# Up's first six blocks interleaved with the row factors, four blocks' weight sums formed in DRAM, and the key scaling moved later

## The chip, the cores and the metric

The kernel runs on one core of one Trainium2 chip. TensorE (PE, with PEld for its weight loads), VectorE (DVE), ScalarE (ACT), GpSimd (POOL) and SyncE (SP) each work through a queue of their own, in order; sixteen DMA engines move data between DRAM and SBUF and within DRAM. SP and POOL here mostly issue transfers. The metric is the device time of one execution, in microseconds (us): 2825.24 us as the median of three runs before the change (2822.13 to 2829.9).

## The reference

One residual block of a decoder, sequence 512, width 2048, everything in float32:

```python
h = rms_norm(x, norm1_g);  z = h @ w_in                    # 2048 -> 9152 columns
o_rw  = rwkv7_mix(token_shift(z[..., :shift]), ...)        # 16 heads of 64, a recurrence over the tokens
o_att = swa_attention(q, k, v, ...)                        # 16 heads, window 128, sinks
x = x + (sigmoid(zg_rw) * (o_rw @ w_branch[:1024]) + sigmoid(zg_att) * (o_att @ w_branch[1024:])) @ w_out
x = x + conv_ffn(rms_norm(x, norm2_g), w_up, conv_w, conv_b, w_down)

def conv_ffn(h, w_up, conv_w, conv_b, w_down):
    u = h @ w_up                                           # 2048 -> 11264
    c = causal 3-tap convolution of u along the tokens, + conv_b
    val, gate = split(c);  return (silu(gate) * val) @ w_down
```

In the RWKV part the keys are scaled to unit length per head: `kk = (k * k_k) / max(sqrt(sum(kk^2)), 1e-12)`, and `kk` and `kk * a` enter the recurrence; the output takes a bonus from `sum(r * k * r_k)`, which does not use `kk`.

## The kernel before

**Precision.** Each float32 product is made of three matmuls. A weight tile `raw` is split into `whi` (an ACT copy, rounded) and `wlo` (a DVE subtraction), the other factor likewise, and PE forms hi·hi, hi·lo and lo·hi. So each 128x1024 weight tile costs one ACT and one DVE instruction besides its load, and PE has 24 matmuls for it in Up.

**Stages in order.** (1) `x` is normalised and transposed. (2) The input projection runs through column tiles (`ztile`, `project`, lines 255 to 257), with attention work first and then eight RWKV pairs (of two heads each). For each pair `early` projects k, r and v and prepares the factors, `late` runs the recurrence (`psG`, `psU`, `psS`), `final` makes the output; gate tiles fill PE in between. (3) The branch projection ends with `factors` and `store_factors`, which write the row factors of the next stage to DRAM. (4) The output projection "o", (5) Up with the convolution, and (6) Down "dn".

**Seven products instead of eight.** Stages 4 to 6 use a Strassen-Winograd scheme: the rows' side and the weights' side are cut in halves, and seven products of sums replace eight. On the weights' side of "o" and "dn" the sums are made in DRAM during earlier stages: `sums_along` takes a job, lets SP copy one quarter to a scratch tensor (SP, pinned in order), and POOL then adds the other by an accumulating transfer. For Up, block f (0 to 43, 256 output columns as two 128-column tiles) needs the products P1, P2, P7, P6, P5, Q4, P3. Their weights are a quarter (P1, P2, Q4) or a sum: s3 for P7 and s1 for P5 are made in SBUF by an SP load and an accumulating POOL transfer, while P6 = a11 + s1 and P3 = P6 + a12 are made by DVE additions in the tile `a` (`sums`, line 1069).

**Rows' side of Up.** After "o" the four quarters q11, q12, q21, q22 of the new x are normalised and transposed. The first two (from the upper rows) become the factors b11 and b21 while "o" still runs. The lower rows come only with the last product of "o": `taken_out` (line 974), squares and sums on ACT, `diagonals` (a 128x128 diagonal of row scales), then `transposed` (line 1024) for q12 and q22. From them come t3 = q22 - q12, t1 = q11 - q12, t2 = -t1 - q22, t4 = -t2 - q21 and b22 = q22, each a 128x2048 DVE operation, and each then split into hi (ACT, line 1040) and lo (DVE, line 1041).

**What sets the order in Up.** The list `steps` gives PE's products. `run(i)` issues the split of the weights of step i+2 (`prep`, lines 1075 and 1076), then the 24 matmuls of step i, then the output instructions (`out`, lines 1109 to 1113). `pin` keeps these in the order of the program; the split of row factors was not pinned, so the scheduler placed it. `whi` and `wlo` have rings of three tiles, so a split can start only when PE has left the product three steps back. Weight tiles have a ring of six (`raw`) and one of two (`a`); a load goes out when the tile's last reader has been prepared. SP's loads and POOL's accumulating transfers each stand in one queue, together with the copies and sums for "dn" that `sums_along` still spreads over Up. Before, the list was: P1, P2, P7 of blocks 0 to 3; then blocks 0 and 1 with P6, P5, P3, Q4 interleaved; the same for 2 and 3; then block by block. P1 and P2 of blocks 0 to 3 are kept in `t1` and in the upper half `Z` of the PSUM tile until the upper rows' output can be placed.

Of the kernel before, what the change touches and what calls it, by code (L numbers as in the profile page):

```python
# [134 lines left out]
def block_kernel(ctx: ExitStack, tc: tile.TileContext, d: Dims, a: dict, out: bass.AP):  # L135
# [18 lines left out]

    ident = const.tile([P, P], F32, name="ident")
# [60 lines left out]
    jobs = []  # L216
    for w in ("o", "dn"):
        for kinds in (
            (("s1", (1, 0), (1, 1)), ("s3", (0, 0), (1, 0))),
            (("s2", "s1", (0, 0)),),  # L220
            (("s4", "s2", (0, 1)),),
        ):
            jobs += [(w, k, c, q) for c in range(NB[w]) for q in range(2) for k in kinds]
    def sums_along():

        if not jobs:
            return lambda: None
        w, (n, first, second), c, q = jobs.pop(0)
        dst = sum_d[w][n][c][q]
        pin(sync.dma_start(dst, quarter(w, first, c)[q], max_dma_last_dim=4096))  # L230
        return lambda: pool.dma_start(dst, quarter(w, second, c)[q], accum_op=ALU.add, max_dma_last_dim=4096)
# [46 lines left out]
    if True:  # L278
# [188 lines left out]
        with ExitStack() as pr:  # L467
# [67 lines left out]
            def early(p):  # L535
# [5 lines left out]

                acc = ztile(d.c_k + p * P)
# [10 lines left out]
                dve.tensor_tensor(kk, kk, rb, op=ALU.mult)  # L553


# [17 lines left out]
                ta = wtile("lw")  # L573
# [219 lines left out]
            for p in range(NP):  # L793
# [3 lines left out]
                final(p, lt)  # L797
                for _ in range(GATES_PER_PAIR * NK // 16):
                    emit_gate()
# [70 lines left out]
    hp = hps.enter_context(tc.tile_pool(name="hhlC", bufs=3, side="right", reuse_waits="tile"))  # L870
# [92 lines left out]
    def taken_out(i, acc, xr, scale, done):  # L963
        ci, tj, sign = PRODUCTS[i][4]
        last = i in (3, 4, 5, 6)
        for t in range(NT // 2):
            for e in range(NQW):
# [5 lines left out]
                else:  # L973
                    dve.scalar_tensor_tensor(x, acc[t][e], sign * scale, x, op0=ALU.mult, op1=ALU.add)
# [6 lines left out]
    bq = {n: [bqp.tile([P, KH, TH], F32R, name=f"{n}{i}") for i in range(2)] for n in ("b11", "b21")}  # L981
    NCC = d.D // S
# [32 lines left out]
    def transposed(tps, i, q, dg=None):  # L1015
# [11 lines left out]
        for k in range(KH):  # L1027
            src, g = pss[k // 2][:, k % 2], col("n2g", i * KH + k)
            dst = q[:, 2 * k // KH, k % (KH // 2) * TH : (k % (KH // 2) + 1) * TH]
            if k % 2:  # L1030
                dve.tensor_scalar(dst, src, g, None, op0=ALU.mult)
            else:
                act.activation(dst, src, AF.Copy, scale=g)
# [4 lines left out]
    def split_q(n, q):  # L1038
        hi, lo = (halves(x) for x in bq[n])
        act.activation(hi, q, AF.Copy)  # L1040
        dve.tensor_tensor(lo, q, hi.bitcast(F32), op=ALU.subtract)
# [3 lines left out]


    NPRE = 4

    class Block:
# [3 lines left out]
        def __init__(self, f):  # L1053
            self.f, self.w, self.hl = f, {}, {}

        def load(self, n):
            f, w = self.f, self.w
            at = {"p11": (0, 0), "p12": (0, 1), "a11": (0, 0), "a12": (0, 1), "s3": (0, 0), "s1": (1, 0), "a22": (1, 1)}
            w[n] = raw_tile("a11", 2) if n in ("a11", "p11") else raw_tile()
            sync.dma_start(w[n], a["w_up"][(f, *at[n])])  # L1060
            if n in ("s3", "s1"):
                pool.dma_start(w[n], a["w_up"][f, 1, int(n == "s1")], accum_op=ALU.add)

        def sums(self, n):

            w = self.w
            if n in ("P6", "P3"):
# [3 lines left out]
        def parts(self, n):  # L1071
            one = "ap"[self.f < NPRE]
            t = self.w[{"P1": one + "11", "P2": one + "12", "P7": "s3", "P6": "a11", "P5": "s1", "Q4": "a22", "P3": "a11"}[n]]
            hi, lo = (hlp.tile([P, WC], F32R, name=f"w{e}", tag=f"w{e}") for e in ("hi", "lo"))
            pin(act.activation(hi, t, AF.Copy))  # L1075
            pin(dve.tensor_tensor(lo, t, hi.bitcast(F32), op=ALU.subtract))  # L1076
            self.hl[n] = hi, lo

        def mm(self, n):
# [6 lines left out]
            ps = getattr(self, {"P2": "Z", "P7": "Y", "Q4": "Y"}.get(n, "X"))  # L1086
            start = n in ("P1", "P7") or n == "P2" and self.f >= NPRE
# [8 lines left out]
        def out(self, n):  # L1096
            X, Y, Z = self.X, getattr(self, "Y", None), self.Z
            if n == "P7":
                return
# [292 lines left out]
```

## Time and profile before

| what | value |
|---|---|
| median of the runs | 2825.24 us (2822.13 to 2829.9) |
| the profiled execution's own time | 2823.84 us |
| its span, first to last instruction | 2822.0 us |
| PE busy | 2768.1 us, 98% of the span |
| DVE busy | 1994.0 us, 71% |
| ACT busy | 1350.7 us, 48% |
| POOL busy | 225.3 us, 8% |
| moved by DMA | 607.04 MB, 215 GB/s over the span |

PE is busy nearly always, so time can come only from the places where it is not, or from making it do less. A row of a window view gives, for a stretch of time, each engine's busy time in it, the granted TensorE clock (1.00 is full speed) and the share of the DMA engines' time in use; what is missing from PE's busy time there is a gap. "[0.88 <-DVE x L974]" after an instruction says how long its engine stood idle before it and what ended the wait. The chain is the path of work that ended last, one piece after the other.

### The profile page before, as it was taken

What the parts mean: (1) busy time and instruction counts of PE and PEld (TensorE: products, weight loads), DVE (VectorE), ACT (ScalarE), POOL (GpSimd) and SP (SyncE); (2) the same over time, 40 slices, a digit from 0 to 9 for tenths busy, and PEclk for the clock granted to TensorE, in tenths of its full rate; (3) what the DMA queues carried; (4) which work ended last, traced back from release to release, by engine and by line L of the source; (5) the groups of instructions that cost most, each with busy time, mean ns of one, the idle gap of its engine ahead of it and who ended that gap; (6) DMA issues with size and microseconds to landing.
All of it is one profiled execution on the core that took longest, in us unless ns stands there. A gap on an engine that the chain in (4) does not pass through costs nothing.

```text
span 2822.0 us, 45987 instructions
## 1 busy us (share of the span) xinstructions
PE 2768.1 (98%) x17466; PEld 2401.8 (85%) x17466; DVE 1994.0 (71%) x3456; ACT 1350.7 (48%) x2274; POOL 225.3 (8%) x299
## 2 busy tenths in 40 slices
PE   7999999999999999999999899999999999999999
PEld 5777787787778778888888899999999999888887
DVE  4588677777777774545678777777777778655555
ACT  4255445544544553322465545554545455444444
POOL 0001000000000001011010010111010101000000
PEclk9999999999999999999999999999999999999999
DMA  7855676666666667888777888888888888877875
GB/s 219 224 158 163 176 183 163 173 170 162 172 165 178 154 168 220 237 258 286 234 251 220 223 224 238 243 228 219 239 237 229 221 241 231 312 243 241 257 256 188
DMA packets 223726, 607.04 MB, mean 215 GB/s; under 512 B 24448, under 2 KB 44560, under 8 KB 222480
## 3 DMA queue, kind: packets, MB, share of 16 engines
q1 hardware_dynamic: 156096, 432.64, 47.5%
q0 software_dynamic: 36064, 132.14, 24.6%
q10 hardware_dynamic: 31344, 39.31, 4.1%
q8 instruction: 137, 2.24, 0.3%
q14 instruction: 85, 0.70, 0.1%
HBM read 554.38 MB, written 174.40 MB: 258 GB/s over the span
## 4 chain that ended last, share of the span: by engine, by line
PE 88%; DVE 5%; ACT 2%; DMA 2%; issue 1%; ACTq 0%; SPq 0%; DVEq 0%; POOLq 0%
PE X L1093 17%; PE X L960 11%; PE acc L256 10%; PE acc L255 10%; PE acc L257 10%; PE Y L960 9%; PE Y L1093 8%; PE Z L1093 4%; PE psS L744 1%; PE psG L735 1%; PE bulk L627 1%; DVE wlo L241 1%; PE bulk L677 1%; DMA raw<-in_w_dn_dram 1%; ACT whi L240 1%
## 5 line engine op out<-in xcount | busy, mean ns | idle before, releaser
L256 PE MATMUL acc<-xlo,whi 128*128 128x512 f32 x1152 | 462.9, 402 | 0.0
L255 PE MATMUL acc<-xhi,whi 128*128 128x512 f32 x1152 | 460.1, 399 | 1.9 <-DVE xlo L301 1.9
L257 PE MATMUL acc<-xhi,wlo 128*128 128x512 f32 x1152 | 461.7, 401 | 0.0
L953 DVE TENSOR_TENSOR wlo<-raw,whi 128x1024 fp32r<-128x1024 f32 x210 | 256.9, 1224 | 207.1 <-ACT whi L952 204.1
L240 ACT ACTIVATE whi<-raw 128x512 fp32r<-128x512 f32 x352 | 220.1, 630 | 364.1 <-PE acc L256 287.9
L952 ACT ACTIVATE whi<-raw 128x1024 fp32r<-128x1024 f32 x210 | 222.8, 1061 | 289.7 <-PE X L960 146.4
L241 DVE TENSOR_TENSOR wlo<-raw,whi 128x512 fp32r<-128x512 f32 x352 | 241.4, 689 | 158.5 <-ACT whi L240 145.2
L1093 PE MATMUL X<-b,whi 128*128 128x256 f32 x1472 | 269.1, 283 | 2.3 <-DVE u L1113 0.9
L1076 DVE TENSOR_TENSOR wlo<-raw,whi 128x1024 fp32r<-128x1024 f32 x176 | 214.9, 1222 | 76.6 <-ACT whi L1075 76.1
L1093 PE MATMUL X<-t,whi 128*128 128x256 f32 x1408 | 258.7, 284 | 9.6 <-DVE u L1113 9.1
L1093 PE MATMUL Y<-t,whi 128*128 128x256 f32 x1408 | 257.1, 283 | 0.0
L255 PEld LDWEIGHTS acc<-xhi,whi 128*128 128x128 f32 x1152 | 217.3, 189 | 42.2 <-DVE xlo L301 2.2
L256 PEld LDWEIGHTS acc<-xlo,whi 128*128 128x128 f32 x1152 | 217.4, 189 | 40.2 <-issue 1.7
L257 PEld LDWEIGHTS acc<-xhi,wlo 128*128 128x128 f32 x1152 | 217.3, 189 | 38.3 <-issue 0.9
L1075 ACT ACTIVATE whi<-a 128x1024 fp32r<-128x1024 f32 x132 | 139.4, 1056 | 215.9 <-DVE a L1069 214.2
L1093 PEld LDWEIGHTS X<-b,whi 128*128 128x128 f32 x1472 | 229.5, 192 | 3.1 <-issue 2.4
L1093 PEld LDWEIGHTS X<-t,whi 128*128 128x128 f32 x1408 | 220.7, 193 | 10.2 <-DVE u L1113 6.6
L1093 PEld LDWEIGHTS Y<-t,whi 128*128 128x128 f32 x1408 | 219.6, 192 | 0.0
L1093 PE MATMUL X<-b,wlo 128*128 128x256 f32 x736 | 208.4, 283 | 2.1 <-DVE wlo L1076 2.1
L1076 DVE TENSOR_TENSOR wlo<-a,whi 128x1024 fp32r<-128x1024 f32 x132 | 161.7, 1225 | 67.6 <-ACT whi L1075 66.9
L1093 PE MATMUL X<-t,wlo 128*128 128x256 f32 x704 | 199.8, 284 | 0.3 <-DVE wlo L1076 0.3
L1093 PE MATMUL Y<-t,wlo 128*128 128x256 f32 x704 | 199.2, 283 | 0.0
(352 smaller groups left out, 5786.1 us busy)
## 6 DMA issues: line engine op xcount, KB each, us to landing
raw<-in_w_up_dram SPq DMA_DIRECT2D x180, 512.0 KB, 5.3
raw<-in_w_z_dram SPq DMA_DIRECT2D x288, 256.0 KB, 4.2
s_dn<-in_w_dn_dram POOLq DMA_DIRECT2D x88, 512.0 KB, 6.6
raw<-in_w_up_dram POOLq DMA_DIRECT2D x88, 512.0 KB, 8.4
raw<-s_dn SPq DMA_DIRECT2D x88, 512.0 KB, 3.9
raw<-in_w_dn_dram SPq DMA_DIRECT2D x66, 512.0 KB, 3.9
a<-in_w_up_dram SPq DMA_DIRECT2D x48, 512.0 KB, 5.3
s_dn<-in_w_dn_dram SPq DMA_DIRECT2D x44, 512.0 KB, 5.3
```

The costliest lines, as they stand in the source:

```text
L240: act.activation(hi, raw, AF.Copy)
L241: dve.tensor_tensor(lo, raw, hi.bitcast(F32), op=ALU.subtract)
L255: pe.matmul(acc, whi[:, j], xhi[:, k], start=first, stop=False)
L256: pe.matmul(acc, whi[:, j], xlo[:, k], start=False, stop=False)
L257: pe.matmul(acc, wlo[:, j], xhi[:, k], start=False, stop=last)
L627: pe.matmul(ps[:, j * 2 * P : (j + 1) * 2 * P], BKK[:, n0 + j], BAR[:, n0 + j].rearrange("p h a c -> p (h a c)"), start=True, stop=True)
L952: act.activation(whi, wr, AF.Copy)
L953: dve.tensor_tensor(wlo, wr, whi.bitcast(F32), op=ALU.subtract)
L960: pe.matmul(dst, l[:, q, ts], r[:, es], start=fst and j == 0, stop=lst and j == 2, skip_group_check=True)
L1075: pin(act.activation(hi, t, AF.Copy))
L1076: pin(dve.tensor_tensor(lo, t, hi.bitcast(F32), op=ALU.subtract))
L1093: pin(pe.matmul(ps, l[:, k], r[:, k], start=start and k + i == 0, stop=last and i == 2, skip_group_check=True))
```

## The change

1. **Sums in DRAM for blocks 0 to 3.** Sixteen new jobs (`up_jobs`: s3, s1, P6, P3 for each block) use the same `sums_along`: one at the beginning of each `early`, one after each `final`. Each is an SP copy of 512 KB in DRAM and an accumulating POOL transfer of 512 KB. P3's copy reads the finished P6, and P6's addition reads s1. Up then loads the finished sums, and the accumulating transfers of s3 and s1 and the DVE additions for P6 and P3 fall away for these four blocks.
2. **Another order of Up's steps**, with P6 of blocks 0 to 3 right after P7, and blocks 4 and 5 interleaved with each other and with the end of blocks 2 and 3. Blocks 2 and 3 take P5 and P3 into `Z` (`apart`).
3. **The row factors written out in that order**, pinned: `high` and `low` replace `split_q` and stand between the steps; t1 comes after t3 and t2. The split of b21 is moved from the end of "o" into Up, and the last weight split before Up is divided (`lo1` after `taken_out`).
4. **Another place for the factor tiles of "o"**: the pool `hhlC` has two tiles, used for the first two; the others (`hhlO`, three tiles) lie on the left side of SBUF, in memory that the branch stage used.
5. **RWKV pairs:** the multiplication of `kk` by its scales `rb` comes after the split of `rk` instead of right after the scales are asked for, so what does not use `kk` stands ahead of it; `ta` and `rk` live in other tiles.

```diff
+    NPRE = 4
+    up_d = {(f, n): dram.tile([P, DH], F32, name=f"{n}_u{f}") for f in range(NPRE) for n in ("s3", "s1", "P6", "P3")}
...
+    jobs, up_jobs = [], []
+    for f in range(NPRE):
+        w, t = a["w_up"][f], {n: up_d[f, n] for n in ("s3", "s1", "P6", "P3")}
+        up_jobs += [(t["s3"], w[0, 0], w[1, 0]), (t["s1"], w[1, 0], w[1, 1]), (t["P6"], w[0, 0], t["s1"]),
+                    (t["P3"], t["P6"], w[0, 1])]
...
+    def sums_along(jobs=jobs):
         if not jobs:
             return lambda: None
+        dst, first, second = jobs.pop(0)
+        pin(sync.dma_start(dst, first, max_dma_last_dim=4096))
+        return lambda: pool.dma_start(dst, second, accum_op=ALU.add, max_dma_last_dim=4096)
...
+                sums_along(up_jobs)()
                 acc = ztile(d.c_k + p * P)
...
                 rb = head_rows(wk, bulk(), rs, "lg")
-                dve.tensor_tensor(kk, kk, rb, op=ALU.mult)
...
-                dve.tensor_tensor(kb, kk, ta, op=ALU.mult)
                 rk = wtile("lw")
                 dve.scalar_tensor_tensor(rk, rz, col("r_k", p), k2, op0=ALU.mult, op1=ALU.mult)
-                rkl = [wk.tile([P, S], F32R, name=f"rk{e}", tag="gn" if e else "lg") for e in range(2)]
+                rkl = [wk.tile([P, S], F32R, name=f"rk{e}", tag="rhl" if e else "dd") for e in range(2)]
                 split(*rkl, rk)
+                pin(dve.tensor_tensor(kk, kk, rb, op=ALU.mult))
+                dve.tensor_tensor(kb, kk, ta, op=ALU.mult)
...
-    hp = hps.enter_context(tc.tile_pool(name="hhlC", bufs=3, side="right", reuse_waits="tile"))
+    hp0 = hps.enter_context(tc.tile_pool(name="hhlC", bufs=2, side="right", reuse_waits="tile"))
...
+    hp = hps.enter_context(tc.tile_pool(name="hhlO", bufs=3, reuse_waits="tile"))
...
+    def high(n, q, pin=pin):
+        pin(act.activation(halves(bq[n][0]), q, AF.Copy))
+
+    def low(n, q, pin=pin):
         hi, lo = (halves(x) for x in bq[n])
-        act.activation(hi, q, AF.Copy)
-        dve.tensor_tensor(lo, q, hi.bitcast(F32), op=ALU.subtract)
+        pin(dve.tensor_tensor(lo, q, hi.bitcast(F32), op=ALU.subtract))
...
+            sync.dma_start(w[n], up_d[f, n] if (f, n) in up_d else a["w_up"][(f, *at[n])])
+            if n in ("s3", "s1") and f >= NPRE:
                 pool.dma_start(w[n], a["w_up"][f, 1, int(n == "s1")], accum_op=ALU.add)
...
+            if n in ("P6", "P3") and self.f >= NPRE:
                 t = w["a11"]
                 pin(dve.tensor_tensor(t, t, w["s1" if n == "P6" else "a12"], op=ALU.add))
...
-    steps = [(f, n) for n in ("P1", "P2", "P7") for f in pre]
-    for f in range(0, NPRE, 2):
-        steps += [(f + e, n) for e, n in ((0, "P6"), (0, "P5"), (1, "P6"), (0, "P3"), (1, "P5"), (0, "Q4"), (1, "P3"), (1, "Q4"))]
-    steps += [(NPRE, "P1")]
+    steps = [(f, n) for n in ("P1", "P2", "P7", "P6") for f in pre]
+    steps += [(0, "P5"), (1, "P5"), (0, "Q4"), (0, "P3"), (1, "Q4"), (1, "P3")]
+    steps += [(4, "P7"), (2, "P5"), (5, "P7"), (2, "Q4"), (3, "P5"), (2, "P3"), (3, "P3"), (3, "Q4")]
+    steps += [(4, "P1"), (4, "P2"), (4, "P6"), (5, "P1"), (4, "P5"), (5, "P2"), (4, "Q4"), (4, "P3")]
+    steps += [(5, "P6"), (6, "P7"), (5, "P5"), (6, "P1"), (5, "P3"), (5, "Q4")]
...
+            loads.append((at - (2 if f >= NPRE and n in ("P7", "P6") else 0), f, "s1" if n == "P6" and f >= NPRE else OF.get(n, n)))
...
+    run(4)
+    high("t3", q12)
+    prep(7)
+    run(5)
+    low("t3", q12)
+    prep(8)
```

In the built program PE has the same 18380 instructions as before, DVE 3458 before and 3454 now, ACT 2335 and 2339, POOL 303 and 311, SP 1118 and 1134. How the order moves is shown at three places.

VectorE, from the copy of the transposed q22 out of PSUM through the formation of t3 and t2 and their splits (q22 is `x_12251` before and `x_12299` now, q12, which becomes t3, `x_12249` and `x_12297`, q11 `x_12248` and `x_12296`; t2 is written over t1 before and over t3 now). Before:

```order
L1031 TENSOR_SCALAR x_12251<-ps_t,par 128x256 x4
L1076 TENSOR_TENSOR wlo<-raw,whi 128x1024
L1253 TENSOR_TENSOR x_12249<-x_12251,x_12249 128x2048
L1263 SCALAR_TENSOR_TENSOR x_12248<-x_12248,x_12251 128x2048
L1041 TENSOR_TENSOR t_15053<-x_12249,t_15052 128x2048
L1076 TENSOR_TENSOR wlo<-raw,whi 128x1024 x3
L1041 TENSOR_TENSOR t_15055<-x_12248,t_15054 128x2048
L1076 TENSOR_TENSOR wlo<-raw,whi 128x1024
L1041 TENSOR_TENSOR b_15049<-x_12251,b_15048 128x2048
```

Now:

```order
L1042 TENSOR_SCALAR x_12299<-ps_t,par 128x256 x4
L1301 TENSOR_TENSOR x_12297<-x_12299,x_12297 128x2048
L1087 TENSOR_TENSOR wlo<-raw,whi 128x1024
L1118 TENSOR_TENSOR t_15161<-t_15161,X 128x256
L1087 TENSOR_TENSOR wlo<-raw,whi 128x1024
L1118 TENSOR_TENSOR t_15196<-t_15196,X 128x256
L1054 TENSOR_TENSOR t_15096<-x_12297,t_15095 128x2048
L1087 TENSOR_TENSOR wlo<-raw,whi 128x1024
L1118 TENSOR_TENSOR t_15257<-t_15257,X 128x256
L1087 TENSOR_TENSOR wlo<-raw,whi 128x1024
L1311 SCALAR_TENSOR_TENSOR x_12297<-x_12296,x_12299 128x2048
```

Before, three 128x2048 operations stood in a row between two weight splits; now at least one weight split stands between any two of them.

SyncE, the loads of Up from its first ones (`s_u` and `P_u` are the new sums in DRAM). Before:

```order
L1060 DMA raw<-in_w_up_dram 128x1024 x6
L1060 DMA a_15008<-in_w_up_dram 128x1024
L1060 DMA a_15014<-in_w_up_dram 128x1024
L1060 DMA a_15217<-in_w_up_dram 128x1024
L1060 DMA a_15348<-in_w_up_dram 128x1024
L1060 DMA raw<-in_w_up_dram 128x1024 x10
```

Now:

```order
L1071 DMA raw<-in_w_up_dram 128x1024 x6
L1071 DMA a_15266<-P_u_148 128x1024
L1071 DMA a_15268<-P_u_152 128x1024
L1071 DMA raw<-s_u_146 128x1024
L1071 DMA raw<-s_u_150 128x1024
L1071 DMA raw<-s_u_154 128x1024
L1071 DMA raw<-s_u_158 128x1024
```

The sums of blocks 0 to 3 now come as plain loads in the order of use.

ScalarE, the first weights of "o" (`whi`) and its row factors (`hhi`). Before:

```order
L952 ACTIVATE whi<-raw 128x1024
L240 ACTIVATE whi<-raw 128x512
L952 ACTIVATE whi<-raw 128x1024 x2
L209 ACTIVATE hhi<-hraw 128x512
L952 ACTIVATE whi<-raw 128x1024 x2
```

Now:

```order
L960 ACTIVATE whi<-raw 128x1024
L248 ACTIVATE whi<-raw 128x512
L960 ACTIVATE whi<-raw 128x1024
L212 ACTIVATE hhi<-hraw 128x512 x3
L960 ACTIVATE whi<-raw 128x1024 x5
```

Three factor splits now stand in a row ahead of the fifth weight of "o"; before, one stood between the fifth and the sixth.

More of the change, by code (lines that the diff above doesn't have):

```diff
@@ L1184, in prep @@
             some_later(1)
-            B[f].parts(nm)
+            lo = B[f].parts(nm)
+            if not split:
+                lo()
             some_later(n - 1)
@@ L1188, in prep @@
             issue_loads()
+            return lo
         else:
```

171 lines of the change are left out of this document (107 added, 64 removed).

## The prediction

> **What bounds the kernel now.** I read the page's busy times first, then windows by stage, then PE's waits and the chain where PE is idle.
>
> ```profile
> PE 2768.1 (98%) x17466; PEld 2401.8 (85%) x17466; DVE 1994.0 (71%) x3456; ACT 1350.7 (48%) x2274; POOL 225.3 (8%) x299
> ```
>
> PE is missing 53.9 us in all (2822.0 - 2768.1). The change adds and removes no matmul, so it can only win back some of these, or open new gaps. In the windows the columns are the stretch, its length, the busy time of PE, PEld, DVE, ACT and POOL, the granted clock, and the DMA share.
>
> ```profile
> 420.00:1110.00 690.00, 683.05 (x4478) 547.44 (x4477) 517.38 (x1262) 335.73 (x743) 56.67 (x77) 1.00 0.67 168
> 1110.00:1315.00 205.00, 205.00 (x906) 169.75 (x905) 98.01 (x161) 60.69 (x100) 24.86 (x36) 1.00 0.85 264
> 1484.77:1652.05 167.28, 154.12 (x1266) 152.97 (x1267) 134.73 (x163) 87.91 (x118) 17.41 (x22) 0.98 0.79 219
> 1550.00:1566.00 16.00, 9.64 (x80) 9.44 (x79) 11.93 (x16) 7.74 (x10) 1.75 (x2) 0.88 0.71 169
> 1566.00:1580.00 14.00, 14.00 (x107) 14.00 (x108) 11.00 (x15) 7.44 (x11) 0.87 (x1) 0.90 0.85 229
> 1652.00:1672.20 20.20, 20.20 (x171) 20.20 (x170) 15.24 (x18) 10.49 (x15) 1.72 (x2) 1.00 0.99 273
> ```
>
> The third row is Up's first 50 products, the stretch that the change reorders: PE is idle for 13.16 us there, a quarter of all. Its waits are these (line waited for, total, times, longest), and the chain through it (start, duration):
>
> ```profile
> PE X L1093 <- DVE u L1113: 10.1, 3, 6.4
> PE X L1093 <- DVE wlo L1076: 2.1, 1, 2.1
> ```
>
> ```profile
> 1477.83 3.28 PE X L960 x14
> ...
> 1481.67 2.35 DVE wlo L1076 x2
> 1484.03 0.61 DVE x L974
> ...
> 1484.77 8.87 PE X L1093 x72
> 1493.64 3.57 PE ps_t L1024 x32
> 1497.22 2.87 PE X L1093 x24
> 1500.09 3.36 PE ps_t L1024 x30
> ...
> 1507.60 2.20 DVE x L1253
> 1509.80 2.02 DVE x L1263
> ...
> 1544.82 4.74 DMA raw<-in_w_up_dram
> ...
> 1550.11 10.97 DMA raw<-in_w_up_dram
> ...
> 1561.10 1.24 DVE a L1069
> ...
> 1565.81 13.11 PE X L1093 x96
> ...
> 1657.81 2.88 PE Z L1093 x24
> ```
>
> There are two mechanisms. Around 1507 the weight split for P7 of block 0 stands behind 128x2048 operations of the row factors on DVE. Around 1550 block 2 waits for a load, then for the accumulating transfer on top of it, then for a DVE addition, and only then for its two splits. After that long gap the granted clock is 0.88 and 0.90, and 96 matmuls take 13.11 us, where four products of 2.88 would be 11.52: 1.59 us more.
>
> **The parts, each worked out.** Durations come from one execution of 2823.84 us (its span and 1.84 us around it), 1.4 us under the median; I add that at the end.
>
> *Step 1, the start of Up.* The last matmul of "o" ends near 1483.9 and P1 begins at 1484.77, after 0.88 us of waiting for `taken_out` (L974), which stood on DVE behind two weight splits (2.35 us from 1481.67) and behind b21's split before them. Now b21's split comes later and one of the two weight splits follows `taken_out`. DVE then follows the banks as PE finishes them: -1.0 us, of which the 0.88 is the wait and 0.1 the slow restart. At worst it stays 0.
>
> *Step 2, Up's first 50 products.* Step 50 of both orders starts after the same set of products, P7 of block 7 being next. Z at 1657.81 is two products later, so before it was 1657.81 - 2 x 2.88 = 1652.05, 167.28 us after P1's start. The work in it is 50 x 2.88 = 144.0 and the transpositions 3.57 + 3.36 = 6.93, together 150.93. So 16.35 us are lost: 13.16 idle, and 3.19 of slow or restarted matmuls (1.59 of them above). How much returns depends on whether the new order keeps every split in time.
>
> ```profile
> L1076 DVE TENSOR_TENSOR wlo<-raw,whi 128x1024 fp32r<-128x1024 f32 x13 | 15.7, 1220 | 2.9 <-ACT whi L1075 2.9
> L1041 DVE TENSOR_TENSOR t<-x,t 128x2048 fp32r<-128x2048 f32 x4 | 9.1, 2286 | 0.8 <-ACT t L1040 0.8
> L1075 ACT ACTIVATE whi<-raw 128x1024 fp32r<-128x1024 f32 x13 | 13.5, 1050 | 3.9 <-PE Y L1093 2.1 <-PE X L1093 1.8
> L1040 ACT ACTIVATE t<-x 128x2048 fp32r<-128x2048 f32 x4 | 7.6, 1910 | 1.6 <-DVE x L1253 1.4
> ```
>
> A ring of three lets a split begin two products, 5.76 us, before its own. ACT's 1.05 and DVE's 1.22 take 2.27 of that and leave 3.49 us. Three large operations in a row (2.20 + 2.02 + 2.29) exceed it by 3.0 us, and the waits of 0.5 and 2.1 us near 1513 are that. Now one large operation, at most 2.29, stands ahead of a weight split on DVE, and 1.91 on ACT: both fit. The tightest place is t2, where a DVE formation (2.2), an ACT copy (1.91), a weight split (1.05 and 1.22) and the low part (2.29) form a chain: I get the weights of step 11 about 0.3 us late. The row scales (`diagonals`) come about 0.5 us after PE has left the first two products. I keep 1.2 us for these and their restarts; the bounds are 0 and, if each of the five factor splits cost its ACT copy again, 5 x 1.91 = 9.5.
>
> The gap at 1550 loses its cause for blocks 0 to 3. Eight accumulating transfers on POOL and eight DVE additions (8 x 1.24 = 9.9 us of DVE) fall away. Four ACT copies out of PSUM and four DVE output additions of about 0.4 us each come instead, beside PE: DVE is busy for 134.73 of 167.28 us there. What is late next are blocks 4 and 5, which still accumulate. The tightest is s3 of block 5: its load goes out when the weights of step 17 are split and its sum is needed before step 24, which is 7 products less the split, about 20.0 us. Load and accumulation cost 5.3 + 8.4 = 13.7 us by the medians below; with the slowest seen, 10.97, and a queue's wait of 0.9 it is 17.2. So 2.8 to 6.3 us are left. Step 2 in all: 1.2 - 16.35 = -15.15.
>
> ```profile
> q1 hardware_dynamic: 156096, 432.64, 47.5%
> q0 software_dynamic: 36064, 132.14, 24.6%
> ...
> raw<-in_w_up_dram SPq DMA_DIRECT2D x180, 512.0 KB, 5.3
> raw<-in_w_z_dram SPq DMA_DIRECT2D x288, 256.0 KB, 4.2
> s_dn<-in_w_dn_dram POOLq DMA_DIRECT2D x88, 512.0 KB, 6.6
> raw<-in_w_up_dram POOLq DMA_DIRECT2D x88, 512.0 KB, 8.4
> ...
> s_dn<-s_dn SPq DMA_DIRECT2D x44, 512.0 KB, 10.0
> ```
>
> *Step 3, sixteen more copies and sums during the RWKV pairs.* Each is an SP copy within DRAM (up to 10.0 us to landing, by the row `s_dn<-s_dn`) and a POOL accumulation (6.6 us). By the queue rows, one 512 KB accumulation took 24.6% x 2822 / (132.14 / 0.524) = 2.75 us of all engines and one copy on q1 1.62, so sixteen make 70 us in the 690 us window: its share rises from 0.67 to about 0.77. Between 1110 and 1315 the share was 0.85 and from 1652 on 0.99, and PE had no gap in either. I take 0, covered by that room; the bound above is the queue rival below. A gain I exclude here, since PE waits for no load in that window. The eight removed accumulations ease Up's start; that too is in step 2.
>
> The Trainium skill, "DMA: Bandwidth & Descriptors", section "Issuing engines are not separate DMA queues", says that transfers issued by any engine share the same 16 DMA engines and interleave, so that a second issuing engine saves only the time of issuing. By that rule the new transfers compete with the `w_z` loads, and the sum would be worse if the room were gone; the rows of 0.85 and 0.99 with no gap speak against it here.
>
> *Step 4, the key scales.* In the first pair PE waits for factors whose DVE work stood behind `kk`, and DVE waited 4.82 us for the scales. The rows are PE's waits from 300 to 420, then one ACT row of the same pair:
>
> ```profile
> PE bulk L627 <- DVE BAR L610: 1.8, 1, 1.8
> PE bulk L627 <- DVE bon L597: 1.5, 1, 1.5
> ```
>
> ```profile
> 322.63 0.42 ACT L209 ACTIVATE wghi<-wl 128x256 fp32r<-128x256 f32 x1 [3.78 <-DMA wl<-in_lora_dram]
> ```
>
> All 3.3 us could go, but the new order still has DVE's share of `wghi`'s split ahead, which cannot start before 322.63. Following DVE's instructions from there, the last piece of BAR ends 0.6 us earlier and `bon` 1.46 us earlier: -1.5 us, bounds 0 and -3.3. In later pairs PE hardly waits; nothing there.
>
> *Step 5, the factor tiles of "o".* Three of them lie where the branch stage kept its rows, released near 1323, and ACT splits three factors in a row ahead of the fifth weight.
>
> ```profile
> 1328.86 1.06 ACT L952 ACTIVATE whi<-raw 128x1024 fp32r<-128x1024 f32 x1 [1.74 <-PE X L960]
> ...
> 1331.67 0.63 ACT L209 ACTIVATE hhi<-hraw 128x512 fp32r<-128x512 f32 x1 [1.75 <-PE X L960]
> ```
>
> The third factor's load has landed by 1331.7, so the fifth weight's ACT copy moves from 1328.86 to about 1333, its DVE half ends near 1335.2, and PE needs it at 1334.9 (12 matmuls at 3.28 / 14 each make 2.81 us a weight). I take +0.4; the bounds are 0, if the load lands 1 us sooner, and 1.5, if 1 us later.
>
> Sum: -1.0 - 15.15 + 0 - 1.5 + 0.4 = -17.25, or 2806.6 by this execution and, with 1.4 for the median, 2808. Its own range: 2802 (nothing kept in step 2, all of step 4) to 2812 (step 1 and step 4 nothing, 1.1 more in step 5).
>
> **Rivals.**
>
> *A sum of block 4 or 5 is late.* Six products are pulled forward against their accumulations, and a load ahead of them in SP may hold them. Then the old gap comes once more, near step 24 or 32: its idle wait of 6.4 less the scheduled room it displaces, say 5.6, and 1.6 of slow clock, 7.2 us: 2815. For it: 10.97 was seen against a median of 8.4. Against it: 2.8 us of room even so.
>
> *The factor splits still delay the weights*: 9.5 us of step 2 return less the 1.2 counted: 2808 + 8.3 = 2816, at the edge of no change. For it: DVE had 134.73 of 167.28 us in use. Against it: the walk above, where one large operation fits.
>
> *Slower: P3's copy stops SP.* P3's copy in SP waits for P6's accumulation, and the `w_z` loads behind it wait too.
>
> ```profile
> POOL s_dn L231 <- DMA s_dn<-in_w_dn_dram: 352.5, 34, 18.4
> ```
>
> That is POOL's longest wait of this kind from 420 to 1110. In the program's order ten `w_z` loads of 2.81 us lie between the two copies, 28 us; copy and sum take 10.0 + 6.6 = 16.6, and a ring of four leaves 4 x 2.81 - 4.2 = 7.0 more. So it decides only if the sum lands over 35 us after its copy is issued. If it came 18.4 us after SP had reached P3's copy, each of four pairs would lose 11.4 us: 2808 + 45.6 = 2853.
>
> *The extra traffic has no room*, as the rule cited would have it if 0.77 were already too much: a `w_z` load late by the 1.62 us of a copy, sixteen times, 26 us: 2834. The rows at 0.85 and 0.99 exclude it nearly.
>
> **How the numbers follow.** Main case 0.64, late sum 0.15, factor splits 0.12, P3's copy 0.05, traffic 0.02, and 0.02 that blocks 0 to 3 wait as before for something else and nothing is gained. A measurement of this kernel tells about 0.3%, 8.5 us, from no change: the bounds are 2816.8 and 2833.7. Main case, late sums and a third of the factor rival are faster: 0.83. The rest of the factor rival and the last case are the same: 0.10. P3's copy and the traffic are slower: 0.07. The range 2802 to 2817 holds the main case, the late sum and half of the factor rival, about 0.83 with some scatter off each end.
>
> **What would show it.** Right: from P1's start to step 50 about 152 us where it was 167; the granted clock at 1.00 throughout; no wait for `u` of 6 us; PE's waits in that stretch near 1 us together; no accumulating load for blocks 0 to 3; the first pair's two waits near 1.8 us together; a small wait near 1334 for "o"; a DMA share near 0.77 in 420 to 1110 with PE still at 683. Wrong: a wait for `raw` of block 4 or 5 in Up, waits for `wlo` at t2 or b22, or waits for `whi` in the RWKV pairs at P3's copies.

## The result, and the profile after

The changed kernel takes 2810.91 us as the median of six runs (2809.11 to 2813.61), against 2825.47 for the kernel before (six runs, 2821.9 to 2829.9): the ratio is 0.9948, 95% interval 0.9936 to 0.9961, so it is 0.5% faster. Forecast were 2808, and 2802 to 2817 as the range. The profiled execution took 2812.58 us with a span of 2810.7, 11.3 us less than the span before. The medians lie 14.6 us apart: the profiled execution of before was 1.6 us faster than its median and the one of after 1.7 us slower than its own, so a comparison of the two profiles covers only 11.3 us.

The busy times of the whole page after, and then the windows that answer to those of before (same columns; the third is again Up's first 50 products):

```profile
PE 2764.8 (98%) x17466; PEld 2403.0 (85%) x17466; DVE 1990.5 (71%) x3452; ACT 1352.5 (48%) x2278; POOL 232.1 (8%) x307
```

```profile
420.00:1110.00 690.00, 680.12 (x4464) 545.18 (x4464) 518.90 (x1259) 335.11 (x741) 65.41 (x86) 1.00 0.74 185
1110.00:1315.00 205.00, 205.00 (x906) 169.78 (x906) 96.43 (x158) 59.77 (x100) 25.92 (x37) 1.00 0.84 261
1485.18:1642.84 157.66, 153.48 (x1264) 151.55 (x1264) 128.07 (x158) 88.99 (x121) 11.41 (x15) 1.00 0.73 206
```

PE's idle time in Up's start fell from 13.16 to 4.18 us (157.66 - 153.48), but in the RWKV window it rose from 6.95 to 9.88. PE is busy for 3.3 us less in all, though it has the same matmuls. All of PE's waits of the changed kernel that are new or belong to the argument (line waited for, total, times, longest):

```profile
PE bulk L783 <- DVE yc L776: 3.3, 8, 0.5
PE bulk L634 <- DVE BAR L616: 2.7, 1, 2.7
...
PE mi L463 <- ACT phi L212: 1.0, 1, 1.0
...
PE X L1104 <- ACT u L1132: 1.4, 1, 1.4
PE X L1104 <- DVE wlo L1087: 1.2, 3, 0.8
...
PE Z L1104 <- DVE wlo L1087: 0.8, 1, 0.8
```

The wait of 6.4 us for `u`, the one for `taken_out` and the one for `bon` are gone; eight short ones for `yc` have come, one in each RWKV pair. The first matmul of "o" and the chain around Up show where the stages now begin:

```profile
1328.32 0.39 PE L968 MATMUL X<-whi,hhi 128*128 128x512 f32 x1
```

```profile
1485.18 5.76 PE X L1104 x48
...
1643.00 2.88 PE Y L1104 x24
```

Set against the rows of before (1323.30, 1484.77 and 1652.05), and with the spans, this gives the account of the two profiles:

| stretch | before, us | after, us | difference |
|---|---|---|---|
| up to the first matmul of "o" | 1323.30 | 1328.32 | +5.0 |
| "o", to P1 of Up | 161.47 | 156.86 | -4.6 |
| P1 to step 50 of Up | 167.28 | 157.82 | -9.5 |
| step 50 to the end | 1169.95 | 1167.7 | -2.2 |
| sum | 2822.0 | 2810.7 | -11.3 |

A row of the chain can begin 0.16 us behind the first matmul of its stage, where the matmul before it still runs. By the matmuls' own starts P1 began at 1485.02 after the change and step 50 at 1651.89 before it, so that "o" won 4.8 us and Up 9.3.

The total comes out near the forecast by other terms than the forecast's: Up won less than 15.15, the part up to "o" lost 5.0 instead of winning 1.5, and "o" won 4.6 where steps 1 and 5 together had 0.6. The last row is scatter for the most part: of the four experiments below that keep the old code from there to the end, three took 1.6 to 1.8 us less than the profile of before for the first 120 products of "dn", and one 1.1 us more.

The row of Up hangs on one execution of the old order, too. The three kernels with padding in the old pool (next part) run the same code in Up as the kernel before. By the matmuls' own starts its first 50 products took 167.1 us in the profile of before and 169.0, 171.0 and 171.5 us in theirs, with a granted clock over the stretch of 0.98, 0.97, 0.96 and 0.95. With the changed kernel's code of that stretch they took 157.8, 157.8 and 157.7 us in three profiles, at 1.00. So Up won 11.9 us on average, and the 9.3 of the pair of profiles is the least of it.

### The profile page after: what moved, and what is told of

It reads as the page before. It is cut to its first block, busy times and chain, and to the rows that moved or that the text cites. A ratio compares the mean times of both kernels' runs of the same rounds, so it can differ in the third digit from the quotient of the medians.

```text
span 2810.7 us, 45990 instructions
## 1 busy us (share of the span) xinstructions
PE 2764.8 (98%) x17466; PEld 2403.0 (85%) x17466; DVE 1990.5 (71%) x3452; ACT 1352.5 (48%) x2278; POOL 232.1 (8%) x307
## 4 chain that ended last, share of the span: by engine, by line
PE 88%; DVE 6%; ACT 3%; issue 1%; DMA 1%; SPq 0%; ACTq 0%; DVEq 0%
PE X L1104 18%; PE X L968 11%; PE acc L264 9%; PE acc L263 9%; PE acc L265 9%; PE Y L1104 9%; PE Y L968 9%; PE Z L1104 4%; DVE wlo L249 1%; PE psS L751 1%; PE bulk L634 1%; PE psG L742 1%; PE bulk L684 1%; ACT whi L248 1%; PE mi L463 1%
## 5 line engine op out<-in xcount | busy, mean ns | idle before, releaser
L961 DVE TENSOR_TENSOR wlo<-raw,whi 128x1024 fp32r<-128x1024 f32 x210 | 257.1, 1225 | 199.7 <-ACT whi L960 199.7
L960 ACT ACTIVATE whi<-raw 128x1024 fp32r<-128x1024 f32 x210 | 222.7, 1061 | 283.8 <-PE X L968 137.0
L1087 DVE TENSOR_TENSOR wlo<-raw,whi 128x1024 fp32r<-128x1024 f32 x184 | 224.8, 1223 | 77.5 <-ACT whi L1085 77.2
L1085 ACT ACTIVATE whi<-a 128x1024 fp32r<-128x1024 f32 x124 | 130.9, 1056 | 201.6 <-DVE a L1080 193.7
L1085 ACT ACTIVATE whi<-raw 128x1024 fp32r<-128x1024 f32 x184 | 192.9, 1049 | 22.8 <-ACT whi L1085 14.1
L1087 DVE TENSOR_TENSOR wlo<-a,whi 128x1024 fp32r<-128x1024 f32 x124 | 152.0, 1226 | 67.5 <-ACT whi L1085 66.9
```

Of the source, the lines that this page charges most:

```text
L960: act.activation(whi, wr, AF.Copy)
L961: dve.tensor_tensor(wlo, wr, whi.bitcast(F32), op=ALU.subtract)
L1087: return lambda: pin(dve.tensor_tensor(lo, t, hi.bitcast(F32), op=ALU.subtract))
```

## The experiments

"Start of o" below is the time of the first matmul of "o"; the steps of Up are counted from 0 in the list `steps`, and the loss of a stretch of steps is its length less 2.88 us a step.

### Why "o" became shorter

In "o" 96 products of 512 columns, one row of the chain each, before and then after the change:

```profile
1390.66 22.40 PE Y L960 x96
```

```profile
1394.12 21.76 PE Y L968 x96
```

That is 233.3 and 226.7 ns a product, without any idle time and at a granted clock of 1.00. The change moved the factor tiles to another pool (part 4). In the built programs (addresses are not in the traces) the factors, the stationary operand, begin 160 bytes past a multiple of 512 per partition before, and at a multiple of 512 now; the weights, the moving operand, begin at a multiple of 512 in both. Three kernels pad the old pool (P is 128, 8 floats are 32 bytes; the other two have 40 and 104):

```diff
     hps = ExitStack()
+    shift = hps.enter_context(tc.tile_pool(name="shift", bufs=1, side="right"))
+    pool.memset(shift.tile([P, 8], F32, name="shift"), 0.0)
     hp = hps.enter_context(tc.tile_pool(name="hhlC", bufs=3, side="right", reuse_waits="tile"))
```

A fourth puts the same 32 bytes ahead of the new pool `hhlO` of the changed kernel.

> The kernel before, with one change: 32 bytes of padding on the right side of SBUF, so that the row factors of "o" (hhlC) start at a multiple of 64 bytes per partition instead of 32 past one; order and work are unchanged. In the kernel before each of the 672 products of 512 columns in "o" came every 233.3 ns, after the change every 226.7 ns once the factors lay in the new pool. Theory, the start address of the stationary operand sets the pace: every 226.7 ns here too, 672 x 6.6 ns = 4.4 us less, about 2821. Rival, the side of SBUF or the number of tiles in the pool: 233.3 ns as before, no difference in time.

> The changed kernel, with 32 bytes of padding ahead of its new pool hhlO, so that the row factors of "o" start 32 bytes past a multiple of 64 as before the change, still on the left side of SBUF. Theory, the address: 233.3 ns a product, 4.1 us more than the changed kernel, about 2815. Rival, the place: 226.7 ns, no difference.

> The kernel before, with 160 bytes of padding in place of 32, so that the row factors of "o" start at a multiple of 512 bytes per partition, still on the right side of SBUF. The run with 32 bytes left them 128 past such a multiple and products at 232.7 ns, so 64 is not the step. The weights of "o", the moving operand, start at a multiple of 512; in the projections both operands lie 96 past one and run at 226.7 ns. Theory, the pace is full when both operands have the same offset within 512 bytes: 226.7 ns, 4.4 us less than before, about 2821. Rival, the side of SBUF or the pool decides: 232 to 234 ns, no difference.

> The kernel before with 416 bytes of padding, so that the row factors of "o" start 256 past a multiple of 512 bytes. If the offset that counts is within 256 bytes, 226.7 ns a product as with 160 bytes of padding; if within 512, 230 ns or more.

The same row of the chain in the four, in this order:

```profile
1390.72 22.32 PE Y L962 x96
```

```profile
1392.62 22.40 PE Y L968 x96
```

```profile
1388.95 21.76 PE Y L962 x96
```

```profile
1390.05 21.76 PE Y L962 x96
```

| kernel | offset of the factors to the weights, within 256 bytes | ns a product | ratio to before |
|---|---|---|---|
| before | 160 | 233.3 | 1 |
| with 32 bytes | 128 | 232.5 | 0.9999 (0.9990 to 1.0008) |
| with 160 bytes | 0 | 226.7 | 0.9983 (0.9974 to 0.9992) |
| with 416 bytes | 0 (256 within 512) | 226.7 | 0.9982 (0.9972 to 0.9992) |
| changed | 0 | 226.7 | 0.9948 (0.9936 to 0.9961) |
| changed, with 32 bytes | 32 | 233.3 | 0.9962 (0.9950 to 0.9975) |

The first theory, an address that is a multiple of 64, fell with the first run: it is one, and the pace hardly moved. The side of SBUF is excluded too, since both paces occur on both sides. What fits all six rows is that the pace is full when stationary and moving operand have the same offset within 256 bytes. Only the stationary side was shifted; that an offset of both together is harmless rests on the projections, where both lie 96 past a multiple of 512 and products come every 227 ns, and was not tried by itself. Two more tiles bear it out. In the changed kernel the first 48 products of "o" still use the old pool, at offset 160: they come every 233.2 ns and the others every 226.7 ns, within one profile. The chain's rows show it, the first 96 products, half of them from the old pool, and the next 96:

```profile
1328.48 22.12 PE X L968 x96
1350.60 21.76 PE Y L968 x96
```

The first 24 products of "dn" use a tile that begins 480 bytes past a multiple of 512, an offset of 224, in the kernels before and after: they come every 233.3 ns (the last ten of them, without idle time), and every 226.7 ns in the two combinations below, where that tile begins at a multiple of 512. The 48 products leave 624, so the place is worth 624 x 6.6 ns = 4.1 us; with the 0.9 us for `taken_out` (step 1) that makes 5.0, of which the stage keeps 4.6.

### What part 5 does in the RWKV pairs

One kernel undoes part 5 in the changed kernel:

```diff
                 rb = head_rows(wk, bulk(), rs, "lg")
+                dve.tensor_tensor(kk, kk, rb, op=ALU.mult)
...
-                ta = wtile("at_")
+                ta = wtile("lw")
...
-                pin(dve.tensor_tensor(kk, kk, rb, op=ALU.mult))
-                dve.tensor_tensor(kb, kk, ta, op=ALU.mult)
```

> The changed kernel with part 5 undone (the key scales multiplied in at once, ta and rk in their old tiles). Theory, part 5 costs time: the wait of about 0.41 us for yc before the transposition of each pair's output (8 times, 3.3 us in all, 0.2 before) goes, and the first pair's 2.7 us wait for BAR goes back to 1.8 + 1.5 with less time at half clock behind it, 0.9 us less: 4 us less in all, about 2807. Rival, the yc waits come from the sixteen added sums on SP and POOL: they stay, and the time is within 1 us of the changed kernel's.

PE's waits of that kernel from 345 to 1120 us, all of them:

```profile
PE bulk L686 <- DVE XIW L213: 5.2, 13, 0.6
PE psS L753 <- DVE UV L749: 0.6, 1, 0.6
PE bulk L785 <- DVE yc L778: 0.2, 1, 0.2
```

The waits for `yc` are part 5's: they are 3.3 us in all six profiles that have part 5 and the changed order, and 0.2 here, where the sixteen sums are still made. "o" starts at 1322.8. The median is 2808.67, ratio 0.9946 (0.9932 to 0.9959): the 2.2 us to the changed kernel lie within the intervals. The expected gain of 4 us was read from one profile; the first pair explains why that was too much. PE's matmuls on BAR there, of the changed kernel, of it with the 32 bytes (the same code up to "o") and with part 5 undone:

```profile
332.74 3.45 PE L634 MATMUL bulk<-BAR,BKK 128*128 128x256 f32 x8 [2.71 <-DVE BAR L616]
```

```profile
329.58 2.47 PE L634 MATMUL bulk<-BAR,BKK 128*128 128x256 f32 x8 [2.19 <-DVE BAR L616]
```

```profile
329.15 1.97 PE L636 MATMUL bulk<-BAR,BKK 128*128 128x256 f32 x8 [2.03 <-DVE BAR L619]
...
333.51 1.99 PE L636 MATMUL bulk<-BAR,BKK 128*128 128x256 f32 x8 [1.47 <-DVE bon L606]
```

In the five profiles of kernels with the changed kernel's code up to "o" (the changed kernel, with 32 bytes, and three of the next parts: without the additions, without the taps, P7 moved), BAR and `bon` together took 2.7, 2.2, 1.8, 2.3 and 2.2 us of waiting; in two of them the wait for `bon` is gone, in three 0.5 us of it is left. In the four profiles with the old code up to there (before, and with 32, 160 and 416 bytes) the two took 3.2, 3.6, 2.3 and 2.4 us. That is 2.2 against 2.9 on average, in ranges that overlap. Behind the longest wait with part 5 the eight matmuls took 3.45 us instead of 1.97. "o" starts at 1328.3, 1325.3, 1323.3, 1324.9 and 1325.3 in them, 1325.4 on average; in the four with the old code at 1323.3, 1323.6, 1323.5 and 1324.6, 1323.7 on average. So parts 1 and 5 cost 1.7 us before "o" on average and not 5.0, which is little against the scatter of the five, and the profile of after is the worst of them. Its wait of 1.0 for `phi` in the attention part stands in none of the other four, though the first combination below has one of 1.9.

### Part 1 alone

The sums are added to the kernel before, and nothing else:

```diff
-            sync.dma_start(w[n], a["w_up"][(f, *at[n])])
-            if n in ("s3", "s1"):
+            made = up_d.get((f, {"a11": "P6", "a12": "P3"}.get(n, n)))
+            sync.dma_start(w[n], a["w_up"][(f, *at[n])] if made is None else made)
+            if n in ("s3", "s1") and f >= NPRE:
...
-            if n in ("P6", "P3"):
+            if n in ("P6", "P3") and self.f >= NPRE:
```

> The kernel before with part 1 alone: the sums for blocks 0 to 3 made in DRAM during the RWKV pairs, the steps and the row factors in the old order. Theory, the gap near 1550 belongs to the load, accumulation and addition of block 2: that wait of 6.4 us and the 1.6 us of slow clock behind it go, the waits near 1513 and 1532 stay; 6 to 8 us less than before, about 2818, and the RWKV pairs as long as before within 0.5 us. Rival, the added transfers cost time in the RWKV pairs: those are 2 to 5 us longer than before and most of the gain is gone. Second rival, without the new order another wait takes the gap's place: less than 4 us gained in Up.

2820.26 us, ratio 0.9983 (0.9974 to 0.9991). Up's first 50 products took 163.8 us, 3.3 us less than in the profile of before, which would be the second rival; but against the other three profiles of the old order they took 5.2 to 7.7 us less, so one profile of each does not settle it. What stands is the wait for `u` at block 2: 3.2 us, where it was 6.3 to 8.3 in the four profiles of the old order. The chain through the old gap shows what took its place:

```profile
1559.53 1.23 DVE wlo L1084
1560.76 0.66 DVE c L1138
1561.42 0.07 DVE u L1121
...
1561.67 0.69 DVE c L1143
1562.36 1.14 DVE wlo L1084
1563.49 0.66 DVE c L1138
1564.16 0.34 DVE u L1121
...
1564.54 10.49 PE X L1101 x74
```

No transfer is in it any more, but PE now waits for an output addition (`u`) that stands on DVE behind weight splits and the convolution of the block before (`c`). The forecast had counted the gap as the transfers' alone.

### Why Up won 9.5 us and not 15

In the changed kernel the first 30 steps lose 1.2 us beyond the 6.93 us of their two transpositions (as before), and the splits of the row factors delay nothing: step 11's weights come 0.2 us late. Then steps 30 to 38, from 1579.54 to 1611.16, take 31.62 us instead of 25.92: 5.70 us lost. The two other profiles with the same code there (with 32 bytes, and with part 5 undone) lose 5.69 and 5.70.

```profile
1579.54 0.40 PE L1104 MATMUL X<-b,whi 128*128 128x256 f32 x2
...
1611.16 0.40 PE L1104 MATMUL Y<-t,whi 128*128 128x256 f32 x2
```

Two causes were looked at, and each kernel leaves one out: the additions of P6 and P3 in blocks 4 and 5, and two taps of the convolution in blocks 2 and 3.

```diff
-            if n in ("P6", "P3") and self.f >= NPRE:
+            if n in ("P6", "P3") and self.f >= NPRE + 2:
```

```diff
                 t = self.c[i]
+                if f in (2, 3):
+                    if part == 1:
+                        pin(act.activation(t, t, AF.Silu))
+                    return
```

> The changed kernel without the four DVE additions that make P6 and P3 of blocks 4 and 5 (left out; PE multiplies a11 in their place). In the changed kernel steps 30 to 38 of Up lose 5.6 us to waits and restarts, with ACT waiting 8.5 us for these additions. Theory A, the additions hold the weight copies on ACT and so the splits: the losses of steps 30 to 38 fall under 2 us, about 2807. Theory B, the convolution of blocks 2 and 3, due in one stretch on DVE and ACT, does it: they stay over 3.5 us, about 2810.

> The changed kernel without two of the three taps of the convolution in blocks 2 and 3 (left out: eight DVE operations of 0.75 us between steps 29 and 33). Theory B, this burst delays the weight splits: the losses of steps 30 to 38 (5.6 us) fall under 2 us, about 2807. Theory A, the additions of blocks 4 and 5 do: they stay over 3.5 us, about 2810.

PE's waits from 1560 to 1612, without the additions and then without the taps:

```profile
PE X L1104 <- DVE wlo L1087: 0.9, 2, 0.8
PE Z L1104 <- DVE wlo L1087: 0.8, 1, 0.8
PE Z L1104 <- ACT whi L1085: 0.3, 1, 0.3
```

```profile
PE X L1104 <- ACT u L1132: 0.3, 1, 0.3
PE X L1104 <- DVE wlo L1087: 0.2, 1, 0.2
```

The loss of steps 30 to 38 is 3.35 us without the additions (2808.97 us, ratio 0.9943) and 0.99 without the taps (2805.34, ratio 0.9934, 0.9920 to 0.9947). The convolution of blocks 2 and 3, due in one stretch because two blocks end within three steps, is the larger part of what holds the splits; the additions cost 2.3 us when both stand there. Neither of the two expected outcomes for the additions (under 2, over 3.5) was met. The two kernels leave out unequal pieces: the taps are eight DVE operations of 0.75 us, 6.0 in all, and three of the additions, 1.2 us each, fall into these steps, 3.7 in all. Per us of DVE work left out they give back 0.8 and 0.6 us. So the stretch holds more work for DVE than fits; that the convolution alone would be too much, or does harm in a way that the additions do not, is not shown.

Four kernels tried to use this. One makes the sums of blocks 4 and 5 in DRAM as well (for f below ND, with a third job per pair), one moves a product without output, P7 of block 5, into the stretch; two combine the first of them, or both, with part 5 undone and all factor tiles at the right offset:

```diff
-    NPRE = 4
+    NPRE, ND = 4, 6
```

```diff
-    steps += [(4, "P7"), (2, "P5"), (5, "P7"), (2, "Q4"), (3, "P5"), (2, "P3"), (3, "P3"), (3, "Q4")]
+    steps += [(4, "P7"), (2, "P5"), (2, "Q4"), (3, "P5"), (2, "P3"), (3, "P3"), (3, "Q4"), (5, "P7")]
...
-            prep(i + 2, 2 if 24 <= i <= 8 * NPRE else 1)
+            prep(i + 2, 2 if 23 <= i <= 29 else 1)
```

> The changed kernel with the sums of blocks 4 and 5 made in DRAM as well (24 jobs instead of 16, a third one per pair after the output), so that no accumulating load and no DVE addition is left in Up's first 38 steps. Theory A (additions): the losses of steps 30 to 38 fall from 5.6 to under 2 us, the RWKV pairs stay as long, about 2807. Theory B (convolution burst): 2809 to 2811. Rival, the eight added sums cost time in the RWKV pairs, where PE would wait for weights: over 2812.

> The changed kernel with one product moved: P7 of block 5, which writes no output, from ahead of block 2's Q4 to behind block 3's Q4, into the stretch where the convolution of blocks 2 and 3 is due; the convolution goes at two pieces a step in steps 23 to 29 instead of 24 to 32, so eight steps at most of that rate become seven and the last end before block 4's P1. Theory B (the convolution burst delays the weight splits, as the run without taps showed: 0.99 us lost in steps 30 to 38 in place of 5.70): the losses of steps 22 to 38 fall from 5.7 to between 2 and 4 us. Rival: the same DVE and ACT work stands in the same stretch and the waits only move, 5 to 6 us.

> The changed kernel with part 5 undone, the factor tiles of "o" and the first of "dn" at multiples of 512 bytes, the sums of blocks 4 and 5 in DRAM, and the convolution at two pieces a step in steps 24 to 30 instead of 24 to 32. By the runs before: 2.2 us for part 5, 2.35 for the sums, about 0.5 for the tiles, up to 1 for the pace: about 2805. Rival, the parts overlap or the traffic costs what the sums win: 2808.

> As the run before, with P7 of block 5 moved behind block 3's Q4 and the convolution at two pieces a step in steps 23 to 29: without the additions of blocks 4 and 5 in that stretch, under 1.5 us lost in steps 22 to 38; about 2803.5. Rival, the waits only move: as the run before.

| kernel | loss of steps 22 to 38, us | start of "o" | median, us | ratio to before |
|---|---|---|---|---|
| changed | 5.70 | 1328.3 | 2810.91 | 0.9948 (0.9936 to 0.9961) |
| six blocks' sums | 3.37 | 1325.8 | 2808.57 | 0.9940 (0.9927 to 0.9952) |
| P7 moved | 4.29 | 1325.3 | 2809.69 | 0.9944 (0.9931 to 0.9957) |
| first combination | 3.36 | 1335.8 | 2811.71 | 0.9956 (0.9943 to 0.9968) |
| second combination | 2.52 | 1328.4 | 2809.23 | 0.9948 (0.9936 to 0.9960) |

None can be told from the changed kernel by its time, and the expectations were mostly missed: the sums of six blocks lose 3.37 us where theory A had under 2, P7 moved loses 4.29 where 2 to 4 was expected, and the combinations, expected near 2805 and 2803.5, took 2811.71 (longer than its rival's 2808) and 2809.23. The combinations win in Up and lose it again before "o", and the way they do shows what part 5 is good for. PE's and DVE's waits of the first combination from 345 to 1120, and DVE in one of those places:

```profile
PE psS L753 <- DVE UV L749: 6.6, 4, 2.4
```

```profile
DVE kk L562 <- DMA rsb<-rsd: 7.3, 4, 2.6
```

```profile
794.38 0.69 DVE L562 TENSOR_TENSOR kk<-kk,rsb 128x512 f32<-128x512 f32 x1 [2.62 <-DMA rsb<-rsd]
794.99 0.42 DVE L595 TENSOR_SCALAR lw<-lw 128x512 f32<-128x512 f32 x1
795.44 0.23 DVE L749 COPY UV<-psU 64x64 f32<-64x64 f32 x1
```

The multiplication of `kk` waits for the load of the key scales `rsb` on DVE, the copy `UV` of the recurrence stands behind it, and PE waits for `UV`. The load is late because it goes out late: it reads 4 KB that a store (`rsd`) puts into DRAM, and SP waits for that store to land. These waits of SP from 345 to 1120, in the kernel before, with part 5 undone (sixteen sums) and in the first combination (24 sums):

```profile
SPq L338 <- DMA rsd<-rsT: 13.5, 7, 2.8
```

```profile
SPq L346 <- DMA rsd<-rsT: 15.0, 7, 3.5
```

```profile
SPq L346 <- DMA rsd<-rsT: 27.1, 7, 5.4
```

The DMA share from 420 to 1110 is 0.67, 0.74 and 0.77 in the three. With part 5 in place and the same 24 jobs (six blocks' sums) SP waits for the store for 23.2 us, and PE not for `UV`; with sixteen sums and without part 5 the wait for `UV` was 0.6 us, once. The profile of the first combination is that of its slowest execution (2817.96 us, of five from 2808.66); in the second, with 24 sums and without part 5 as well, PE's wait for `UV` is 2.5 us. So part 5 covers a late load of the scales; whether that is worth the 3.3 us for `yc` with 24 sums, these profiles do not settle.

## Why the prediction was right or wrong

The direction and the range were right, and 2810.91 is near 2808, but in part by luck: terms that were too large or of the wrong sign met one that was not in the sum. The lower end of the main case's own range does not follow from its terms either: 2808 less the 1.2 of step 2 and 1.8 more in step 4 is 2805, not 2802. By its steps:

- **Step 1, right.** The 0.9 us wait for `taken_out` is gone.
- **Step 2, right in what goes, too large in what it brings.** 9.5 us in the pair of profiles, 11.9 on average over the old order's four, instead of 15.15. The step that failed is the sentence that one large operation stands ahead of a weight split and both fit: it walked the factor splits and left out the convolution, which stands in the same queues. It was seen as a busy total of DVE, 134.73 of 167.28 us, and not as work that comes due in one stretch. That stretch costs 5.70 us. The factor splits themselves fit as worked out, and no accumulating load of blocks 4 and 5 was late. The rival "the factor splits still delay the weights" named the right engine and the wrong work; what came, 6 us, is two thirds of its price.
- **Step 2's second mechanism, mis-sized.** Without its transfers the gap of block 2 was still 3.2 us long; with the new order as well it is gone. The new order without the sums in DRAM was not run.
- **Step 3, right with a condition.** The DMA share rose from 0.67 to 0.74 (0.77 forecast) and PE waits for no `w_z` load in the pairs. P3's copy did not stop SP. The cover is thinner than 0.85 and 0.99 suggested: those stretches contain no store and load of the key scales, and these came later with every step of the share. The rule of the Trainium skill cited there ("DMA: Bandwidth & Descriptors", "Issuing engines are not separate DMA queues"), that all transfers share the same engines, is in line with SP's wait for the 4 KB store: 13.5 us with no added sums, 15.0 to 16.8 with sixteen (three profiles) and 21.5 to 27.1 with 24 (three). But SP issues the sums' copies as well, and no run here tells the shared engines from the place in SP's queue.
- **Step 4, wrong in sign.** In the first pair the waits are 0.7 us shorter on average (2.2 against 2.9, five profiles against four), half of the 1.5 forecast, which came from one profile of the old code. "In later pairs PE hardly waits; nothing there" failed: the matmuls on `rk` moved ahead, PE reached the output's transposition 0.4 us before `yc` was ready, eight times, 3.1 us more. That sign is the waits'; the times with and without part 5, 2.2 us apart, do not settle it.
- **Step 5, wrong.** The order of ACT's copies cost nothing in this profile (0.8 us in that of the kernel with part 5 undone, near the 0.4 forecast). The place of the tiles, taken as a matter of when they come free, shortened each product from 233.3 to 226.7 ns, about 4 us in all. With it fell the sentence at the start that the change could only win back idle time: the pace of a busy PE changed.

So the forecast missed 5.7 us of new waits in Up and about 3 us in the pairs, and a gain of 4 us in "o" that it did not know of offset much of it. With the averages, 1.7 us lost before "o", 4.8 won in it and 11.9 in Up make 15.0, near the 14.6 of the medians.

## What to carry to other kernels

When splits or loads are checked against a slack, walk every instruction of the engine's queue through the stretch, outputs included, and ask which blocks end together; a share of busy time hides that. When a tile moves to another pool, compare its address with that of the operand it meets, and look at the time per product of a PE that is never idle. Before a wait of half a microsecond is explained, see whether it stands in a second profile of the same code: here 1.0 us for `phi` did not and 3.3 us for `yc` did. A gain that is the difference of two profiles carries the scatter of both: the old order of Up took 167 to 171.5 us.

## What the runs showed of the hardware that was not expected

- Products of 128x128 by 128x512 in float32 took 226.7 ns when both operands had the same offset within 256 bytes and 232.5 to 233.3 ns at the other offsets that occurred (32, 128, 160 and 224), with PE not idle and a clock of 1.00.
- A wait of PE for 2.0 us cost nothing more (eight matmuls in 1.97 us), one of 2.19 or 2.71 us was followed by slower ones (2.47 and 3.45 us). The window from 325 to 340 us of the changed kernel has a granted clock of 0.89:

```profile
325.00:340.00 15.00, 12.29 (x48) 9.82 (x47) 13.86 (x27) 5.21 (x12) 1.63 (x2) 0.89 0.92 242
```

That length alone does not decide it, three further profiles show, the kernel before with 32 bytes of padding, part 1 alone and the second combination:

```profile
330.94 1.96 PE L627 MATMUL bulk<-BAR,BKK 128*128 128x256 f32 x8 [2.13 <-DVE BAR L610]
```

```profile
331.03 2.79 PE L633 MATMUL bulk<-BAR,BKK 128*128 128x256 f32 x8 [2.13 <-DVE BAR L616]
```

```profile
330.99 2.80 PE L636 MATMUL bulk<-BAR,BKK 128*128 128x256 f32 x8 [1.89 <-DVE BAR L619]
```

The Trainium skill, "TensorE: Matmul & The Clock Gate", "Part 1: The HAM clock gate", puts the drop to half clock after an idle window of about 3.4 us and says that this window runs freely. The waits here are shorter than that by themselves; that 1.89 us was followed by the drop, and 2.13 us once and not the other time, is what a freely running window could do, but no run here set it.
